# A two-layer hybrid diffusion block on one Trainium2 core: the prologue's loads, engine orders and first norm rearranged

## Chip, core and metric

One core of one Trainium2 chip runs the whole program in one launch. The metric is the device time of an execution in microseconds (us). TensorE multiplies (PE in the rows; PEld loads its weights), VectorE is DVE, ScalarE is ACT, GpSimd is POOL; SyncE (SP) only issues DMAs. A q behind an engine's name (SPq, ACTq) marks work of its sequencer.

## What is computed

Two layers over 256 context tokens and 256 latent tokens, D = 1024, all in float32. Cut to what the change touches:

```python
h = rmsnorm(x, norm_mix[i]) * (1 + sc1) + sh1        # sc1, sh1: silu(c) @ w_mod, per stream
... = split_in(h @ w_in[i])                          # three mixers and gates read h
# Hyena's filter, a function of the weights alone:
h = sin(fr * (emb @ w1 + b1)); h = sin(fr * (h @ w2 + b2))
h = (h @ w3) * exp(-t * decay)
k = concatenate([h[:, 0], 0, h[:0:-1, 1]])
k = k / sum(|k|);  k_f = rfft(k)
```

The rest (recurrent scan, Hyena convolutions, SSD, projections, SwiGLU, final norm) is the same in both kernels.

## The kernel before

Weights come as 128x1024 tiles (`wst`), are split into a high part `whi` (ScalarE) and a low part `wlo` (VectorE), and are multiplied with the split activations `hhi`, `hlo`; a planner (`Flow`) walks a list of weight tiles and steps the generators (`gens_step`) that do everything else between the products. A generator gives up the engine with `yield n`, so lags such as `FILT_LAG` set where its pieces stand. The order that results on each engine is a list in which every instruction waits for its operands; a scheduler may move instructions against the written order where nothing ties them.

Before the first weight tile of layer 0 stands a prologue (in `run`, under `if l == 0`):

- `silu_c`: silu of c, for both streams.
- `g_filters` and `filt`: two small sine layers (`sin_rr`, result `h2` in tile `nr`), then for each of four filter parts jp (tiles `w0` to `w3`, one PSUM pool each) four blocks `n`. A block is: ScalarE makes exp(decay), TensorE multiplies `h2` with `w3` of the part, VectorE multiplies the two, ScalarE takes the absolute value, VectorE adds it up. Then eight VectorE sums and differences, the sum over all taps (`ones` products, `kcol`), and five products with the cosine and sine basis `kbas`, copied by ScalarE and stored by a GpSimd DMA (`kd`).
- `mods0`: 16 tiles of `w_mod0` (`wm`) times silu(c), giving `modt` (shift and scale).
- `g_sumsq`: ScalarE squares x (`yc` context, `yl` latent) in 16 pieces, GpSimd adds them up in `nacc` (14 adds).
- `g_norm`: from `nacc` by TensorE, ScalarE (Sqrt) and VectorE (RECIPROCAL) the factor `rc`, spread over the partitions by TensorE; then per stream 8 pairs of VectorE operations with a ScalarE operation between them make `hhi` and `hlo`.

After that the first tiles, D and B0, are multiplied (`f.tile(2)`), and the filters' remains are drained. All loads of the prologue go through SyncE's queue, in this order: small constants, filter inputs, three tiles of `w_mod0`, x, the other 13 tiles (a ring of four).

An issue of a DMA on SyncE or ScalarE takes the next of eight completion counters (DMAHW0 to DMAHW7), whichever engine issues it, and waits until the DMA before it on the same counter has landed. GpSimd's have eight of their own (DMASW0 to 7).

Of the kernel before, what the change touches and what calls it, by code (L numbers as in the profile page):

```python
# [9 lines left out]
F32 = mybir.dt.float32  # L10
F32R = mybir.dt.float32r
AF = mybir.ActivationFunctionType
# [10 lines left out]
LATE = 2  # L23
FILT_LAG = ((2, 2, 0, 1, 1, 0, 2, 1), (8, 7, 1, 3, 2, 0, 4, 3))
MODSTEP = ((2, 2, 4, 3), (3, 2, 2, 2, 1, 1))
PREP_LAG = (17, 12)
MODLAGS = (3, 16, 6)
ORDER_A = ('D B0 C0 B1 C1 X0 X1 X2 X3 R0 R1 X4 X5 Z0 Z1 G0 G1 R2 R3 X6 X7 Z2 Z3 G2 G3 R4 R5 Z4 Z5 G4 G5 R6 R7 Z6 Z7 G6 G7 T20 T21', 'D B0 C0 B1 C1 X0 X1 X2 X3 R1 X4 R0 X5 Z0 G0 Z1 G1 R2 R3 X6 X7 Z2 Z3 H00 G2 G3 H01 R4 R5 Z4 Z5 G4 G5 H10 H11 R6 R7 Z6 Z7 G6 G7 H20 H21 T20 T21')
ORDER_B = ('H00 H20 H10 H01 H11 T22 H21 W20 H12 H02 W21 T23 H22 H03 H13 W22 T24 H04 H14 W23 H23 H24 H05 H15 T25 W24 T26 H25 H06 H16 W25 H17 T27 H26 H07 W26 H27 W27', 'H02 H03 H12 H13 H22 H23 W20 T22 W21 T23 W22 T24 W23 T25 W24 T26 H04 H05 W25 H15 T27 W26 W27 T00 H24 H14 H25 T01 W00 T02 W02 W01 H06 H07 T03 T04 W03 H16 H17 T05 T06 W05 H26 H27 W04 T07 W06 W07')
P = 128  # L30
# [177 lines left out]
class Block:  # L208
    def __init__(self, tc, a, out, es):
        self.tc = tc  # L210
        self.nc = tc.nc
        self.a = a
        self.out = out
        self.es = es
        self.f = Flow(self)
        self.ring = (3, 2)
        self.l = 0
        self.table, self.before, self.group = None, [], []

    def pool(self, name, bufs=1, space=None, es=None):  # L220
# [9 lines left out]
    def mm(self, out, lhsT, rhs, start=True, stop=True):  # L230
        self.nc.tensor.matmul(out=out, lhsT=lhsT, rhs=rhs, start=start, stop=stop)  # L231

# [36 lines left out]
    def tt(self, out, in0, in1, op, eng=None):  # L269
        (eng or self.nc.vector).tensor_tensor(out=out, in0=in0, in1=in1, op=op)  # L270

    def stt(self, out, in0, scalar, in1, op0, op1):
        self.lastop = self.nc.vector.scalar_tensor_tensor(out=out, in0=in0, scalar=scalar, in1=in1, op0=op0, op1=op1).ins.name  # L273

    def ts(self, out, in0, s1, op0, s2=None, op1=None):
        if op1 is None:
            self.nc.vector.tensor_scalar(out=out, in0=in0, scalar1=s1, scalar2=None, op0=op0)
        else:
            self.nc.vector.tensor_scalar(out=out, in0=in0, scalar1=s1, scalar2=s2, op0=op0, op1=op1)

# [73 lines left out]
    def silu_c(self):  # L354

        t = self.t
        self.sil = t(self.cp, [P, KT, 2], "sil")
        self.act(self.sil.rearrange("p k s -> p s k"), self.cs.rearrange("p (s k) -> p s k", s=2), AF.Silu)
        silc = self.t(self.wm, [P, KT, 32], "silc")
        self.nc.vector.memset(silc, 0.0)  # L360
        self.act(silc[:, :, 0:2], self.sil)
        self.silc = silc

        row = t(self.base, [P, T], "btmp", bufs=3)[0:4]
        self.nc.sync.dma_start(out=row, in_=self.a["crow"])
        self.act(row, row, AF.Silu)
        self.sild = t(self.dram, [4, T], "sild")
        self.nc.sync.dma_start(out=self.sild, in_=row)

# [5 lines left out]
    def mods0(self, qs):  # L375

        todo = [(q, k) for q in qs for k in range(KT)]
        sts = []

        def load(i):  # L380
            if i < len(todo):
                st = self.t(self.wm, [P, KT * P], "wm", bufs=4)
                self.nc.sync.dma_start(out=st, in_=self.a["w_mod0"][todo[i][0], todo[i][1]])
                sts.append(st)

        ahead = 3
        for i in range(ahead):
# [59 lines left out]

    def rms_r(self, sq_sum, n, f=1.0, keep=True):

        nb = n // P  # L450
        ps = self.pc()
        for b in range(nb):
            self.mm(ps[:, b:b + 1], sq_sum[:, b * P:b * P + P], self.ones[:, 0:1])
        rc = self.t(self.base, [P, 4], "rc")
        self.act(rc[:, 0:nb], ps[:, 0:nb], AF.Sqrt, bias=self.epsc, scale=f / D)
        self.nc.vector.reciprocal(out=rc[:, 0:nb], in_=rc[:, 0:nb])
        ps = self.pc()
        for b in range(nb):
            self.mm(ps[:, b * P:b * P + P], rc[:, b:b + 1].to_broadcast([P, P]), self.ident)
        if not keep:  # L460
            return ps
        r = self.t(self.base, [P, T], "nr")
        self.act(r[:, 0:n], ps[:, 0:n])
        return r
# [16 lines left out]
    def g_sumsq(self, x, acc):  # L481
        yield 6
        for k in range(KT):
            self.sq_acc(acc, k, [x[0][:, k], x[1][:, k]], eng=self.nc.gpsimd)
            yield 1

    def g_norm(self, l, xs, mi, acc, qsh, wname, out, wait=None):
# [11 lines left out]
        if not wait:  # L499
            r = self.rms_r(acc, NTOK * len(xs), keep=False)  # L500
        for s, x in enumerate(xs):
            sl = slice(s * NTOK, s * NTOK + NTOK)
            if wait:
                if s:
                    yield wait, s
                ra = self.rms_r(acc[:, sl], NTOK, keep=False)[:, 0:NTOK]
            else:
                ra = r[:, sl]
            for k in range(KT):
                tmp = self.t(self.base, [P, T], "btmp", bufs=3)[:, 0:NTOK]  # L510
                sh = mod[:, qsh, k, mi[s]:mi[s] + 1]
                self.stt(tmp, x[:, k], am[:, k, mi[s]:mi[s] + 1], ra, ALU.mult, ALU.mult)
                self.act(hi[:, k, sl], tmp, AF.Identity, bias=sh)
                self.stt(lo[:, k, sl], tmp, sh, hi[:, k, sl].bitcast(F32), ALU.add, ALU.subtract)
                if k % 2:
                    yield 1
        if qsh:
            self.after = self.lastop
            self.f.mark(("normed", l))
# [447 lines left out]
    def sin_rr(self, x, q, outs):  # L967

        big = 12582912.0
        self.ts(q, x, 1.0 / (2.0 * math.pi), ALU.mult)  # L970
        self.ts(q, q, big, ALU.add)
        self.ts(q, q, big, ALU.subtract)
# [7 lines left out]
    def g_filters(self, l, fp, sets=None):  # L980
# [4 lines left out]
        emb = t(fp, [P, T], "emb")[0:33, 0:NTOK] if one else t(fp, [33, NTOK], "emb")  # L985
        self.wmq.dma_start(out=emb, in_=a["emb"])
        w1 = t(fp, [33, 64], "fw1")
        self.wmq.dma_start(out=w1, in_=a["hy_w1"][l])
        w2 = t(fp, [64, 64], "fw2")
        self.wmq.dma_start(out=w2, in_=a["hy_w2"][l])  # L990
        kbas = t(fp, [P, 5, P], "kbas")
# [48 lines left out]
    def filt(self, l, jp, fp, kbas, h2, sl, ks, pool, ptag):  # L1040
# [17 lines left out]
        for n, (d, ti) in enumerate(((0, 0), (0, 1), (1, 0), (1, 1))):  # L1058
# [7 lines left out]
            h = hv[ti, d]  # L1066
            if n == 0 and self.fspl:
                self.act(s0[0:1], ps[0:1])
                for b in range(4):
                    nc.sync.dma_start(out=kc[:, 8 + b:9 + b], in_=s0[0:1, b * P:b * P + P])  # L1070
            if ti == 0:
# [24 lines left out]
        for b in range(4):  # L1096
            self.mm(pt[:, b:b + 1], acc[:, b * P:b * P + P], self.ones[:, 0:1])
            if not self.fspl:
                self.mm(pt[:, 4 + b:5 + b], w3[:, b * P:b * P + P], h2[:, 0, 0:1])
        inv, cb, k0 = kc[:, 0:4], kc[:, 4:8], kc[:, 8:12]  # L1100
        if not self.fspl:
            self.act(k0, pt[:, 4:8])
        self.act(inv, k0, AF.Abs)
# [335 lines left out]
    def run(self):  # L1439
# [9 lines left out]
        for l in range(DEPTH):  # L1449
# [8 lines left out]
            with ExitStack() as ls:  # L1458
# [6 lines left out]
                if l == 0:  # L1465
                    self.wm = self.pool("wm0", es=st)
                    self.wmq = nc.sync
                    self.silu_c()
                    fp = self.pool("fl0", es=st)
                    sets = []  # L1470
                    for i in range(4):
                        w = t(fp, [P, 11, T], f"w{i}")
                        sets.append(([w[:, k] for k in range(6)], w[:, 6:11]) +
                                    ((self.ps_a, "a"), (self.ps_c, "c"), (self.ps_mm, "mm"), (self.ps_mm, "mm"))[i])
                    f.spawn(self.g_filters(0, fp, sets))
                    f.gens_step()
                    g = f.spawn(self.mods0((1, 0)))
                    f.gens_step()
                    for s in range(2):
                        nc.sync.dma_start(out=x[s], in_=self.a["x"][s])  # L1480
                    sq = f.spawn(self.g_sumsq(x, acc))
# [3 lines left out]
                if l == 0:  # L1485
                    f.spawn(self.g_norm(0, x, (0, 1), acc, 0, "norm_mix", self.h_tiles))
                f.drain([g[0] for g in f.gens])
                f.drain(self.fgens)
                st.close()
                self.sb, self.mh, self.ml, self.vh, self.vl = {}, [], [], {}, {}  # L1490
                if last:
                    self.hp_pool = self.pool("hp", es=ls)
                with self.tc.tile_pool(name=f"ssd{l}", bufs=1) as self.ssd_pool, \
# [15 lines left out]
                    if last:  # L1509
                        self.spawn_parts(0, (0, 1), n)  # L1510
                    f.tile(2)
                    f.run(("gt", 2, 1))
# [221 lines left out]
```

## Time and profile before

| | us |
|---|---|
| median of three runs (2065.45 to 2067.81) | 2066.91 |
| the profiled execution's own time | 2069.64 |
| its span, first to last instruction | 2067.9 |
| TensorE busy | 1989.1 (96%) |
| VectorE busy | 1497.8 (72%) |
| ScalarE busy | 1021.3 (49%) |
| GpSimd busy | 275.1 (13%) |

Busy times are unions of the instructions of an engine over the span; matmuls are pipelined and their ends are modelled, so 96% does not say that TensorE runs at its peak. "Idle before" names what ended a wait. Times in the rows count from the first instruction.

### The profile page before, as it was taken

Reading aid. Unit: us, or ns where it says so; the run is one execution under the profiler, and the core shown is the slowest. Engines: PE = TensorE matmul, PEld = TensorE weight load, DVE = VectorE, ACT = ScalarE, POOL = GpSimd, SP = SyncE. Lnnn points to the kernel's source line nnn. Section 1 sums busy time; section 2 is a strip of 40 time slices with the busy share of each in tenths; the row PEclk is TensorE's granted clock in tenths of the full one; section 3 lists DMA queues with packets and bytes.
Section 4 is the critical chain, followed back from the end, with each engine's and each line's share of the span. In section 5 each row is a group of like instructions: output and inputs, shape, how many; then the busy total and the mean of one; then the engine's idle time right before and its main releaser. Section 6 shows DMA issues by size and latency. Waiting matters only on the chain.

```text
span 2067.9 us, 30071 instructions
## 1 busy us (share of the span) xinstructions
PE 1989.1 (96%) x11564; PEld 1693.7 (82%) x11564; DVE 1497.8 (72%) x2422; ACT 1021.3 (49%) x1602; POOL 275.1 (13%) x330
## 2 busy tenths in 40 slices
PE   7999899899999999999999999999999899999998
PEld 3797767678888887888877888897767899999998
DVE  7786765697777789469988455787676898765555
ACT  6556658752222323344424435556768644455444
POOL 3103232220000112011121000003242110000000
PEclk9999999999999999999999999999999999999999
DMA  7621122243232377345686423532233565455563
GB/s 270 221 82 60 60 71 67 87 153 115 89 100 82 123 264 258 109 133 193 204 289 236 133 88 108 152 93 92 79 96 108 186 208 167 154 188 155 184 184 112
DMA packets 84743, 297.15 MB, mean 144 GB/s; under 512 B 12650, under 2 KB 13894, under 8 KB 83193
## 3 DMA queue, kind: packets, MB, share of 16 engines
q1 hardware_dynamic: 61208, 208.40, 31.6%
q0 software_dynamic: 22848, 86.32, 12.6%
q8 instruction: 91, 1.49, 0.3%
q10 hardware_dynamic: 544, 0.52, 0.1%
q14 instruction: 52, 0.42, 0.1%
HBM read 278.41 MB, written 16.79 MB: 143 GB/s over the span
## 4 chain that ended last, share of the span: by engine, by line
PE 72%; issue 9%; DVE 7%; ACT 4%; DMA 4%; POOL 2%; SPq 0%; POOLq 0%; DVEq 0%; ACTq 0%
PE mm L231 61%; PE c L231 6%; PE b L231 3%; PE a L231 2%; DMA wm<-in_w_modt 2%; DVE wlo L270 1%; PE c L246 1%; ACT L259 1%; ACT r L259 1%; POOL r L270 1%; POOL wm L422 1%; DVE r L942 1%; DVE w L270 1%; ACT whi L259 1%; DVE r L937 1%
## 5 line engine op out<-in xcount | busy, mean ns | idle before, releaser
L259 ACT ACTIVATE whi<-wst 128x1024 fp32r<-128x1024 f32 (+1 forms) x374 | 392.5, 1050 | 524.9 <-PE mm L231 423.0
L270 DVE TENSOR_TENSOR wlo<-wst,whi 128x1024 fp32r<-128x1024 f32 (+1 forms) x374 | 456.6, 1221 | 250.2 <-PE mm L231 121.0
L231 PE MATMUL mm<-hhi,whi 128*128 128x256 f32 (+1 forms) x1552 | 504.9, 345 | 14.8 <-DVE u L273 6.8
L231 PE MATMUL mm<-hlo,whi 128*128 128x256 f32 (+1 forms) x1552 | 490.8, 336 | 0.2
L231 PE MATMUL mm<-shi,whi 128*128 128x256 f32 (+1 forms) x1104 | 351.1, 338 | 3.2 <-ACT shi L259 3.2
L231 PE MATMUL mm<-slo,whi 128*128 128x256 f32 (+1 forms) x1104 | 350.9, 338 | 1.7 <-DVE slo L270 0.7
L231 PEld LDWEIGHTS mm<-hhi,whi 128*128 128x128 f32 x1552 | 294.8, 190 | 53.1 <-issue 17.1
L231 PEld LDWEIGHTS mm<-hlo,whi 128*128 128x128 f32 x1552 | 295.4, 191 | 34.8 <-issue 7.9
L231 PE MATMUL mm<-hhi,wlo 128*128 128x256 f32 (+1 forms) x1552 | 304.0, 336 | 0.1
L231 PEld LDWEIGHTS mm<-hhi,wlo 128*128 128x128 f32 x1552 | 241.0, 189 | 32.5 <-issue 5.2
L231 PEld LDWEIGHTS mm<-shi,whi 128*128 128x128 f32 x1104 | 210.4, 192 | 26.6 <-ACT shi L259 5.2
L231 PEld LDWEIGHTS mm<-slo,whi 128*128 128x128 f32 x1104 | 210.7, 192 | 24.3 <-DVE slo L273 1.7
L231 PE MATMUL mm<-shi,wlo 128*128 128x256 f32 (+1 forms) x1104 | 213.7, 336 | 0.9 <-DVE wlo L270 0.9
L231 PEld LDWEIGHTS mm<-shi,wlo 128*128 128x128 f32 x1104 | 174.4, 192 | 22.2 <-DVE wlo L270 1.4
L437 DVE SCALAR_TENSOR_TENSOR wmp<-wm,silr 128x1024 f32<-128x1024 f32 x128 | 156.0, 1219 | 20.8 <-DMA wm<-in_w_modt 19.9
L231 PE MATMUL mm<-vl,whi 128*128 128x256 f32 (+1 forms) x508 | 156.7, 330 | 0.0
L231 PE MATMUL mm<-vh,whi 128*128 128x256 f32 (+1 forms) x508 | 156.2, 330 | 0.0
L231 PEld LDWEIGHTS mm<-vl,whi 128*128 128x128 f32 x508 | 96.4, 190 | 9.9 <-DVE vl L270 0.2
L259 ACT ACT_TABLE_LOAD x78 | 100.1, 1283 | 8.9 <-PE c L231 5.3
L231 PEld LDWEIGHTS mm<-vh,whi 128*128 128x128 f32 x508 | 96.2, 190 | 9.8 <-ACT vh L259 0.6
L231 PE MATMUL mm<-vh,wlo 128*128 128x256 f32 (+1 forms) x508 | 97.5, 332 | 0.0
L231 PEld LDWEIGHTS mm<-vh,wlo 128*128 128x128 f32 x508 | 79.3, 192 | 9.6
(322 smaller groups left out, 2670.8 us busy)
## 6 DMA issues: line engine op xcount, KB each, us to landing
wst<-in_w_in SPq DMA_DIRECT2D x170, 512.0 KB, 3.6
wst<-in_w_up SPq DMA_DIRECT2D x88, 512.0 KB, 3.6
wm<-in_w_modt POOLq DMA_DIRECT2D x80, 512.0 KB, 4.8
wst<-in_w_branch SPq DMA_DIRECT2D x48, 512.0 KB, 3.6
wst<-in_w_down SPq DMA_DIRECT2D x32, 512.0 KB, 3.6
ks<-kd POOLq DMA_DIRECT2D x16, 640.0 KB, 7.1
wst<-in_w_out SPq DMA_DIRECT2D x18, 512.0 KB, 3.6
wm<-in_w_mod SPq DMA_DIRECT2D x16, 512.0 KB, 4.7
```

The lines of the kernel that those rows point to most:

```text
L231: self.nc.tensor.matmul(out=out, lhsT=lhsT, rhs=rhs, start=start, stop=stop)
L246: self.nc.tensor.transpose(out, in_, self.ident[0:n, 0:n])
L259: ins = self.nc.scalar.activation(out=out, in_=in_, func=func, **kw).ins
L270: (eng or self.nc.vector).tensor_tensor(out=out, in0=in0, in1=in1, op=op)
L422: self.nc.gpsimd.dma_start(out=st, in_=self.a["w_modt"][l, todo[i][0], todo[i][1]])
L437: ins = self.nc.vector.scalar_tensor_tensor(out=out, in0=sts[i], scalar=1.0, in1=self.silr[:, s], op0=ALU.mult, op1=ALU.mult, accum_out=do ...
L937: nc.vector.tensor_tensor_scan(out=h, data0=av, data1=i[:, 0], initial=0.0, op0=ALU.mult, op1=ALU.add)
L942: nc.vector.tensor_tensor_scan(out=h[:, sl][:, ::-1], data0=av[:, sl][:, ::-1], data1=i[:, 1, sl][:, ::-1], initial=ini, op0=ALU.mult, op1 ...
```

## The change

Parts, in the order of the program:

1. x is loaded first, by ScalarE's queue; `kbas`, the filter's `w3` and decays too (`wmq = nc.scalar`). SyncE's queue keeps the small constants and `w_mod0`; 12 tiles of it are issued ahead of use instead of 3, eight of them into the space of `hlo` and `hhi`, which nothing uses yet. The store of `sild` goes to GpSimd's queue.
2. In the prologue every matmul is tied behind the one written before it, and every VectorE operation made by `tt`, `stt`, `ts` too (`told`, `chain`): these two engines follow the written order. Lags change.
3. `rms_r` of layer 0 moves to the end of `g_sumsq`, its result is copied to a tile `r0`.
4. `g_norm` writes its second VectorE operation one step later; it is run after three steps and drained, and the filter parts 2 and 3 wait for the norm of stream 0 and 1 before their sums. D and B0 are multiplied inside the prologue, before the filters are drained.
5. `sin_rr` does its multiply and add in one operation (two instead of three).
6. The filter's tap 0 (`k0`) is copied from the first block's product by ScalarE and spread over partitions by four GpSimd DMAs per part, instead of four `nr` x `w3` products per part.

The diff, cut to its core:

```diff
+NORM_LAG = 3
-FILT_LAG = ((2, 2, 0, 1, 1, 0, 2, 1), (8, 7, 1, 3, 2, 0, 4, 3))
+FILT_LAG = ((1, 2, 0, 4, 1, 0, 1, 1), (8, 7, 1, 3, 2, 0, 4, 3))
-PREP_LAG = (17, 12)
-MODLAGS = (3, 16, 6)
+PREP_LAG = (14, 12)
+MODLAGS = (1, 16, 6)
...
+    def chain(self, engine, made):
+
+        if self.told is not None:
+            if engine in self.told:
+                self.order(made.ins, self.told[engine])
+            self.told[engine] = made.ins.name
+        return made
...
-        self.nc.sync.dma_start(out=self.sild, in_=row)
+        self.nc.gpsimd.dma_start(out=self.sild, in_=row)
...
+        big = [self.t(self.base, [P, KT, T], tag).rearrange("p (i k) n -> p i (k n)", i=4) for tag in ("hlo", "hhi")]
+        room = [b[:, i] for b in big for i in range(4)]
...
-                st = self.t(self.wm, [P, KT * P], "wm", bufs=4)
+                st = room[i - 4] if 4 <= i < 12 else self.t(self.wm, [P, KT * P], "wm", bufs=4)
...
-        ahead = 3
+        ahead = 12
...
+        self.r0 = self.rms_r(acc, T, out=self.t(self.wm, [P, T], "r0"))
...
-            r = self.rms_r(acc, NTOK * len(xs), keep=False)
+            r = self.r0
...
-        self.ts(q, x, 1.0 / (2.0 * math.pi), ALU.mult)
-        self.ts(q, q, big, ALU.add)
+        self.ts(q, x, 1.0 / (2.0 * math.pi), ALU.mult, big, ALU.add)
...
-            if n == 0 and self.fspl:
+            if n == 0:
                 self.act(s0[0:1], ps[0:1])
                 for b in range(4):
-                    nc.sync.dma_start(out=kc[:, 8 + b:9 + b], in_=s0[0:1, b * P:b * P + P])
+                    (nc.sync if self.fspl else gp).dma_start(out=kc[:, 8 + b:9 + b], in_=s0[0:1, b * P:b * P + P])
...
+        if not self.fspl and jp > 1:
+            yield ("normed0", jp - 2)
...
-            if not self.fspl:
-                self.mm(pt[:, 4 + b:5 + b], w3[:, b * P:b * P + P], h2[:, 0, 0:1])
...
-                    self.wmq = nc.sync
+                    self.wmq = nc.scalar
+                    for k in range(2):
+                        nc.scalar.dma_start(out=x[k], in_=self.a["x"][k])
...
-                    for s in range(2):
-                        nc.sync.dma_start(out=x[s], in_=self.a["x"][s])
...
-                    f.spawn(self.g_norm(0, x, (0, 1), acc, 0, "norm_mix", self.h_tiles))
+                    for i in range(NORM_LAG):
+                        f.gens_step()
+                    nm = f.spawn(self.g_norm(0, x, (0, 1), acc, 0, "norm_mix", self.h_tiles))
+                    f.drain([nm])
+                    f.tile(2)
```

What moves, at two places. First ScalarE at the start of the program. Before, it issues no DMA, and the first sine layer's Sin (`w_141<-w_141`) is its fifth ACTIVATE:

```order
L259 ACT_TABLE_LOAD
L259 ACTIVATE sil<-cs 128x2x8
L259 ACTIVATE btmp<-btmp 4x512
L259 ACTIVATE silc<-sil 128x8x2
L259 ACTIVATE sp_sc<-sp_nl 128x16
L259 ACTIVATE w_141<-w_141 64x256
L259 ACTIVATE nr<-w_141 64x256 x2
L259 ACT_TABLE_LOAD
```

With the change (the Sin is now `w_146<-w_146`; w_146, w_143, w_145, w_144 are the four filter parts; the counter that each waits for in brackets):

```order
L1014 DMA kbas<-in_kbas 128x640 [waits DMAHW4_49]
L1059 DMA w_146<-in_hy_w 128x512 [waits DMAHW5_49]
L1060 DMA w_146<-in_hy_decay 128x1024 [waits DMAHW7_49]
L1059 DMA w_143<-in_hy_w 128x512 [waits DMAHW1_49]
L1060 DMA w_143<-in_hy_decay 128x1024 [waits DMAHW2_49]
L1059 DMA w_145<-in_hy_w 128x512 [waits DMAHW4_49]
L1060 DMA w_145<-in_hy_decay 128x1024 [waits DMAHW6_49]
L1059 DMA w_144<-in_hy_w 128x512 [waits DMAHW0_49]
L1060 DMA w_144<-in_hy_decay 128x1024 [waits DMAHW1_49]
L269 ACTIVATE w_146<-w_146 64x256 [waits DVE_49]
```

Nine DMA issues now stand in ScalarE's list ahead of that Sin (two for x ahead of these, as the very first). The counters behind the brackets: DMAHW7 is held by the latent half of x, DMAHW1 and DMAHW2 by the second and third tile of `w_mod0`, DMAHW6 by the fifth, DMAHW0 by the context half of x, then the first tile and then the sixth.

Second GpSimd, between the loads and the store of the first filter part. Before:

```order
L321 DMA pp_87<-in_cols 128x336
L321 DMA pp_90<-in_cols 128x336
L270 ISA
L270 TENSOR_TENSOR nacc<-nacc,btmp 128x256 x14
L1125 DMA kd_111<-w_141 128x2560
```

With the change:

```order
L381 DMA sild<-btmp 4x512
L280 ISA
L280 TENSOR_TENSOR nacc<-nacc,btmp 128x256 x2
L1092 DMA kcol_119<-w_146 128x1x1 x4
L1092 DMA kcol_119<-w_143 128x1x1 x4
L1092 DMA kcol_119<-w_145 128x1x1 x4
L1092 DMA kcol_119<-w_144 128x1x1 x4
L280 TENSOR_TENSOR nacc<-nacc,btmp 128x256 x12
L1145 DMA kd_111<-w_146 128x2560
```

The sixteen issues for `k0`, which need the first block of every filter part, stand between the second and the third add of `nacc`.

## Rows read from the trace of the kernel before

**Rows 1.** Stretches: busy time (instructions) of each engine, PEclk granted clock.

```profile
core 0: us, PE busy (x) PEld busy (x) DVE busy (x) ACT busy (x) POOL busy (x), PEclk, DMA share, GB/s
0.00:10.00 10.00, 1.44 (x3) 0.57 (x4) 4.50 (x16) 2.87 (x6) 1.98 (x7) 1.00 0.63 176
10.00:20.00 10.00, 5.70 (x15) 1.68 (x14) 4.37 (x10) 5.95 (x10) 0.00 (x0) 1.00 1.03 415
...
60.00:70.00 10.00, 8.97 (x14) 3.39 (x14) 6.10 (x15) 4.56 (x9) 0.00 (x0) 0.66 0.64 223
...
80.00:90.00 10.00, 10.00 (x76) 9.76 (x75) 5.96 (x13) 4.44 (x9) 1.37 (x3) 1.00 0.64 252
...
160.00:170.00 10.00, 10.00 (x60) 8.21 (x59) 6.43 (x7) 7.59 (x12) 4.59 (x4) 1.00 0.17 52
...
14.85:85.07 70.22, 66.07 (x345) 34.20 (x345) 58.90 (x116) 48.87 (x100) 16.71 (x18) 0.93 0.71 268
```

**Rows 2.** Timeline, 2 to 17 us: start, length, engine, operation [idle before].

```profile
2.39 0.22 ACT L259 ACTIVATE sil<-cs 128x16 f32<-128x16 f32 x1 [0.37 <-DMA cs<-in_cc]
...
9.17 0.42 ACT L259 ACTIVATE w<-w 64x256 f32<-64x256 f32 x1 [4.06 <-DVE w L279]
...
13.99 0.86 ACT L259 ACTIVATE nr<-w 64x256 f32<-64x256 f32 x2 [4.41 <-DVE w L279]
...
14.87 1.28 ACT L259 ACT_TABLE_LOAD   x1
...
16.16 1.95 ACT L259 ACTIVATE w<-w,misc 128x512 f32<-128x512 f32 x3
```

**Rows 3.** SyncE's queue, 0 to 90 us: what its issues waited for, us, times, longest.

```profile
SPq L383 <- DMA w<-in_hy_decay: 2.3, 2, 1.4
```

**Rows 4.** DMA queues in the last 14 us, where SyncE and ScalarE both issue.

```profile
q1 hardware_dynamic: 544, 0.52, 11.3%
q10 hardware_dynamic: 544, 0.52, 11.0%
```

**Rows 5.** Tile nacc, 0 to 95 us: ns min/median/max of one, first and last start.

```profile
L270 POOL TENSOR_TENSOR nacc<-nacc,btmp x14: 722/1174/1245, 26.7 to 47.5; 128x256 f32<-128x256 f32 x14
```

**Rows 6.** GpSimd's groups, 0 to 95 us: busy, mean ns of one, idle before.

```profile
L1125 POOL DMA_DIRECT2D kd<-w x4 | 2.2, 545 | 31.1 <-ACT w L259 31.1
```

**Rows 7.** Timeline, 48 to 77 us: the norm's factor, and the first tile's first product.

```profile
48.13 1.16 PE L231 MATMUL c<-ones,nacc 128*128 128x1 f32 x8
...
49.42 1.28 ACT L259 ACT_TABLE_LOAD   x1
...
50.71 0.26 ACT L259 ACTIVATE rc<-c,epsc 128x4 f32<-128x4 f32 x1
...
66.96 0.17 DVE L456 RECIPROCAL rc<-rc 128x4 f32<-128x4 f32 x1
...
75.85 0.68 PE L231 MATMUL mm<-hhi,whi 128*128 128x256 f32 x1
```

**Rows 8.** Timeline of VectorE, 36 to 85 us: sums, low parts, first and last norm step.

```profile
36.13 2.48 DVE L270 TENSOR_TENSOR w<-w 128x512 f32<-128x512 f32 x4
...
64.61 2.36 DVE L270 TENSOR_TENSOR wlo<-wst,whi 128x1024 fp32r<-128x1024 f32 x2
...
71.15 1.26 DVE L273 SCALAR_TENSOR_TENSOR btmp<-yc,am,c 128x256 f32<-128x256 f32 x3 [4.02 <-PE c L231]
...
84.59 0.48 DVE L273 SCALAR_TENSOR_TENSOR hlo<-btmp,modt,hhi 128x256 fp32r<-128x256 f32 x1 [0.18 <-ACT hhi L259]
```

**Rows 9.** Tile w, 0 to 92 us: ScalarE's operations and the basis products.

```profile
L259 ACT ACTIVATE w<-w x17: 416/614/631, 9.2 to 55.7; 128x512 f32<-128x512 f32 x16, 64x256 f32<-64x256 f32 x1
L259 ACT ACTIVATE w<-w,misc x16: 705/707/722, 16.2 to 48.7; 128x512 f32<-128x512 f32 x16
L259 ACT ACTIVATE w<-mm x10: 582/597/598, 61.5 to 75.6; 128x512 f32<-128x512 f32 x10
```

**Rows 10.** Chain that ended last, 0 to 160 us: start, length, what.

```profile
77.73 0.94 PE c L231 x2
...
79.51 0.98 PE c L231 x2
80.49 12.19 PE mm L231 x94
92.67 0.39 PE c L246 x4
```

More of the change, by code (lines that the diff above doesn't have):

```diff
@@ L218, in __init__ @@
         self.table, self.before, self.group = None, [], []
+        self.told = None
     def pool(self, name, bufs=1, space=None, es=None):
@@ L230, in mm @@
     def mm(self, out, lhsT, rhs, start=True, stop=True):
-        self.nc.tensor.matmul(out=out, lhsT=lhsT, rhs=rhs, start=start, stop=stop)
+        self.chain("PE", self.nc.tensor.matmul(out=out, lhsT=lhsT, rhs=rhs, start=start, stop=stop))
     def mm3(self, out, lhsT, rhs):
@@ L269, in tt @@
     def tt(self, out, in0, in1, op, eng=None):
-        (eng or self.nc.vector).tensor_tensor(out=out, in0=in0, in1=in1, op=op)
+        made = (eng or self.nc.vector).tensor_tensor(out=out, in0=in0, in1=in1, op=op)
+        if eng is None:
+            self.chain("DVE", made)
     def stt(self, out, in0, scalar, in1, op0, op1):
-        self.lastop = self.nc.vector.scalar_tensor_tensor(out=out, in0=in0, scalar=scalar, in1=in1, op0=op0, op1=op1).ins.name
+        made = self.nc.vector.scalar_tensor_tensor(out=out, in0=in0, scalar=scalar, in1=in1, op0=op0, op1=op1)
+        self.lastop = self.chain("DVE", made).ins.name
     def ts(self, out, in0, s1, op0, s2=None, op1=None):
         if op1 is None:
-            self.nc.vector.tensor_scalar(out=out, in0=in0, scalar1=s1, scalar2=None, op0=op0)
+            self.chain("DVE", self.nc.vector.tensor_scalar(out=out, in0=in0, scalar1=s1, scalar2=None, op0=op0))
         else:
-            self.nc.vector.tensor_scalar(out=out, in0=in0, scalar1=s1, scalar2=s2, op0=op0, op1=op1)
+            self.chain("DVE", self.nc.vector.tensor_scalar(out=out, in0=in0, scalar1=s1, scalar2=s2, op0=op0, op1=op1))
     def col(self, name, i=0, n=1, rows=P):
@@ L445, in mods, with rms_r @@
                 self.tt(self.modts[l][:, q, :, s0:2], dot[:, :, s0:2], b, ALU.add)
-    def rms_r(self, sq_sum, n, f=1.0, keep=True):
+    def rms_r(self, sq_sum, n, f=1.0, keep=True, out=None):
         nb = n // P
@@ L461, in rms_r @@
             return ps
-        r = self.t(self.base, [P, T], "nr")
+        r = self.t(self.base, [P, T], "nr") if out is None else out
         self.act(r[:, 0:n], ps[:, 0:n])
@@ L508, in g_norm @@
                 ra = r[:, sl]
[L509 to L514, printed above, removed]
+            tmps = []
+            for k in range(KT + 1):
+                if k < KT:
+                    tmp = self.t(self.base, [P, T], "btmp", bufs=3)[:, 0:NTOK]
+                    tmps.append(tmp)
+                    sh = mod[:, qsh, k, mi[s]:mi[s] + 1]
+                    self.stt(tmp, x[:, k], am[:, k, mi[s]:mi[s] + 1], ra, ALU.mult, ALU.mult)
+                    self.act(hi[:, k, sl], tmp, AF.Identity, bias=sh)
+                if k:
+                    sh = mod[:, qsh, k - 1, mi[s]:mi[s] + 1]
+                    self.stt(lo[:, k - 1, sl], tmps[k - 1], sh, hi[:, k - 1, sl].bitcast(F32), ALU.add, ALU.subtract)
                 if k % 2:
                     yield 1
+            if not wait:
+                self.f.mark(("normed0", s))
         if qsh:
@@ L985, in g_filters @@
         emb = t(fp, [P, T], "emb")[0:33, 0:NTOK] if one else t(fp, [33, NTOK], "emb")
-        self.wmq.dma_start(out=emb, in_=a["emb"])
+        (self.wmq if one else nc.sync).dma_start(out=emb, in_=a["emb"])
         w1 = t(fp, [33, 64], "fw1")
-        self.wmq.dma_start(out=w1, in_=a["hy_w1"][l])
+        (self.wmq if one else nc.sync).dma_start(out=w1, in_=a["hy_w1"][l])
         w2 = t(fp, [64, 64], "fw2")
-        self.wmq.dma_start(out=w2, in_=a["hy_w2"][l])
+        (self.wmq if one else nc.sync).dma_start(out=w2, in_=a["hy_w2"][l])
         kbas = t(fp, [P, 5, P], "kbas")
@@ L1097, in filt @@
             self.mm(pt[:, b:b + 1], acc[:, b * P:b * P + P], self.ones[:, 0:1])
-            if not self.fspl:
-                self.mm(pt[:, 4 + b:5 + b], w3[:, b * P:b * P + P], h2[:, 0, 0:1])
         inv, cb, k0 = kc[:, 0:4], kc[:, 4:8], kc[:, 8:12]
-        if not self.fspl:
-            self.act(k0, pt[:, 4:8])
         self.act(inv, k0, AF.Abs)
@@ L1473, in run @@
                         sets.append(([w[:, k] for k in range(6)], w[:, 6:11]) +
-                                    ((self.ps_a, "a"), (self.ps_c, "c"), (self.ps_mm, "mm"), (self.ps_mm, "mm"))[i])
+                                    ((self.ps_mm, "mm"), (self.ps_a, "a"), (self.ps_c, "c"), (self.ps_mm, "mm"))[i])
+                    sets = [sets[i] for i in (3, 0, 2, 1)]
+                    self.told = {}
                     f.spawn(self.g_filters(0, fp, sets))
@@ L1485, in run @@
                 if l == 0:
-                    f.spawn(self.g_norm(0, x, (0, 1), acc, 0, "norm_mix", self.h_tiles))
+                    for i in range(NORM_LAG):
[3 more added lines that the diff above has]
+                    f.tile(2)
                 f.drain([g[0] for g in f.gens])
                 f.drain(self.fgens)
+                self.told = None
                 st.close()
@@ L1510, in run @@
                         self.spawn_parts(0, (0, 1), n)
-                    f.tile(2)
+                    if last:
+                        f.tile(2)
                     f.run(("gt", 2, 1))
```

## The prediction

> **What bounds the kernel now.** I read the time by stretches first. From 80 us on TensorE is busy in the whole of every 10 us up to 170 us (the first and the last of these nine stretches stand in [rows 1]; the seven between read 10.00 too), so a prologue that ends later or sooner moves everything behind it by about as much. The prologue is another matter: VectorE has 4.50 and 4.37 us of work in the first two stretches of ten. So I followed its start in the timeline [rows 2]: the Sin of the first sine layer stands at 9.17, that of the second is through at 14.85, the table for Exp at 16.15, the first decay factor at 16.16. Then came the waits and the DMA queues [rows 3, 4], GpSimd's adds [rows 5], the factor of the norm [rows 7], VectorE's pace [rows 8], and last the chain [rows 10]: the first product of a weight tile starts at 75.85, and tiles D and B0 with all that remains of the filters end at 92.67. My question is when the changed kernel reaches these two points.
>
> **The change, step by step.**
>
> *1. ScalarE is held up by its own DMA issues.* The change puts nine of them ahead of the first Sin, and the last ones wait for counters held by weight tiles of SyncE's queue. That an issue stands still for a counter is seen on SyncE: twice, 2.3 us in all [rows 3]. The issue of the last part's w3 needs the sixth tile of w_mod0 to have landed. First the two halves of x pass, 2.10 MB: at the 415 GB/s of the stretch from 10 to 20 us, whose DMA share of 1.03 says that the engines are full [rows 1], 5.1 us, from a first issue at about 0.7 and 1.6 us to landing as for cs (0.74 to 2.39) [rows 2], some 7 us. Six tiles are 3.15 MB. Where SyncE's and ScalarE's queues ran side by side they had 11.3% and 11.0% [rows 4], an equal share; at half of 415 the tiles take 15.2 us and end at 22, at the full rate 7.6 us and end at 15. ScalarE's queue is empty for part of the time, since its own issues wait, but not for most: I take 21. The Sin goes from 9.17 to 21.3: 12 us late (bounds 6 and 13, and 0 if a waiting issue didn't hold the engine: a rival below).
>
> Beside this row stands the Trainium skill, "DMA: Bandwidth & Descriptors", section "Issuing engines are not separate DMA queues": transfers issued by different engines share the same 16 DMA engines and interleave, and a second issuer only saves issue time. By it, part 1 of the change gains no bandwidth, which the equal shares agree with; if it gained some, the 21 would be nearer 15.
>
> *2. Up to the first decay factors.* From the first Sin to the end of the second took 5.7 us [rows 2]; one VectorE operation on 64x256 falls away in it, for which I take 0.3 (ScalarE's Sin on as many elements takes 0.42). So h2 is there at 26.7, and with 1.28 us for the table Exp begins at 28.0, 12 us late. All filter inputs have landed by then or soon after, the last being issued at 21.5.
>
> *3. First blocks.* ScalarE now does an Exp (0.71, 0.61 to the next) and a copy of tap 0 for each of four parts. The copy has no row: one partition of 512 elements lies between nothing and the 0.60 of a 128x512 copy [rows 9]; I take 0.5, nearest to the latter since the length is the same. Four pairs: 4.5 us, so the fourth copy is through at 32.8, the first at 29.2.
>
> *4. GpSimd.* Sixteen issues of about 0.54 us [rows 6] follow the first copy: 29.3 to 38. Behind them stand twelve adds of 0.72 to 1.25 us [rows 5]: through at 46.7 to 53. The longer ones belong to stretches in which VectorE was busy, and it now waits; I take 1.0 and 50. Before, the last add began at 47.5. ScalarE's squares share three buffers with these adds and stand in its list between the Exps, so the later blocks go at GpSimd's pace.
>
> *5. The norm's factor.* In the written order TensorE's product with nacc stands ahead of the fourth part's third block, and VectorE's RECIPROCAL ahead of its multiply. So VectorE stops there until nacc is complete: 1.16 for the products, 0.26 for the Sqrt, hand-overs of about 0.8 [rows 7], RECIPROCAL at 52.2 (before: 66.96, where nothing but the norm waited for it). The table goes back to Exp (1.28), an absolute value and an Exp follow, then VectorE's multiply: through at 56.
>
> *6. VectorE from there to the third part's last sum.* Counted in its list: 36 operations on 128x512 at 0.62 (four in 2.48), two low parts in 2.36, 23 of the norm's 32 steps at 0.435 (32 from 71.15 to 85.07), 13 small ones at 0.1 [rows 8]: 22.3 + 2.4 + 10.0 + 1.3 = 36 us, to 92.
>
> *7. TensorE from there.* Three basis products of 0.9 (two passes took 0.94 and 0.98 [rows 10]) with ScalarE's copies beside them stand ahead of tile D: first product at 94.5, against 75.85. That is **18.7 us late**.
>
> *8. Inside tiles D and B0* the changed kernel still has seven basis products and four with ones to do, the kernel before two: five times 0.9 and four of 0.22 make **5.2 us**. The sums of the fourth part, which they wait for, come within the time that the products take.
>
> *9. Behind them* ScalarE's list now has the split of a third weight tile ahead of the copy of tile D, which waits for another tile's products; 1.06 and 0.6 us and two hand-overs, **about 2 us** (0 to 2.5).
>
> *10. TensorE's clock.* In 60 to 70 us the granted clock was 0.66 of full, two thirds of that stretch at 1.2 GHz [rows 1], behind a stretch with waits. The changed kernel leaves TensorE without work for longer, some 8 us ahead of step 7: **1 us** (0 to 4).
>
> Gains, all hidden: 16 products of tap 0 fewer on TensorE (3.5 us), which waits anyway; x and w_mod0 there earlier, which nothing on the new path waits for except through step 1. The shift and scale leave the path.
>
> Sum: 18.7 + 5.2 + 2 + 1 = 27 us, nothing of it caught up later. Against the profiled execution's 2069.64, which is 2.7 above the median, that is 2096.6; against the median of 2066.91 it is **2094 us**. The bounds: adds at 0.72 and the sixth tile at 18 give 20 us, 2087; adds at 1.25, hand-overs in every dependent pair of sums (0.1 each, some 2 us) and 4 us of slow clock give 36 us, 2103.
>
> **Rivals.**
>
> *A. ScalarE isn't held up by waiting issues.* Then h2 is ready at 14.5, but the fourth part's decay still comes behind 5.6 MB of its own queue and as much of the other: about 27 us. The fourth copy ends near 29, its four issues near 31, the adds at 43, RECIPROCAL at 45: 7 us sooner than in the forecast, +20, 2087. For it: an issue is no work of the engine that the rows count as busy. Against it: rows 3 show SyncE's list in order behind a waiting issue. The Trainium skill, "Perfetto Trace Analysis", section "DMA Instruction — HWDGE (DVE, Sync)", has the semaphore wait in the sequencer, which is free for its next instruction only after the issue; by it this rival falls and the sum stands. Chance 0.12.
>
> *B. Faster: VectorE's gaps close.* From 14.85 to 85.07 VectorE was idle for 11.3 us (70.22 less 58.90 [rows 1]). If inputs come early enough, the written order fills half of that, and the fourth part's eight sums (5.0 us at 0.62) come behind the norm instead of ahead: tile D starts 10.6 us earlier, less 5.2 of step 8: 5 us gained, 2062. It decides at ScalarE's last issue: it would have to leave before about 9 us, with GpSimd's adds done by 44. Six tiles and x by then are 5.2 MB in 7 us, 750 GB/s, where rows 1 show 415. Chance 0.08.
>
> *C. The delay is made up* in the tile stage: 2067. Against it: TensorE has no gap there to give back [rows 1]. Chance 0.05.
>
> **How the numbers follow.** The forecast has 0.75. Rival A lies inside its range. 2079 to 2104 takes in its bounds, A, and a case between A and B in which both holds are shorter than priced. A measurement of this kernel tells about 0.2%, 4 us, from no change. Faster by more than that: B, 0.08. Within it: C, 0.05. Slower: 0.87.
>
> **What would show each step.** The first Sin near 21 us with DMA issues ahead of it on ScalarE; the first Exp near 28; sixteen issues on GpSimd and nacc's last add ending near 50; RECIPROCAL of rc near 52 with VectorE idle before it; the first tile product near 95 and the end of D and B0 near 117. A first Sin at 9 to 10 would leave A or B; nacc complete before 44 would take most of the rest away. A first tile product before 75 would make the forecast wrong as a whole.

## Result and profile after

The changed kernel takes 2091.36 us (median of four runs, 2089.10 to 2099.88) against 2067.36 (2065.45 to 2078.11): ratio 1.0124, 95% interval 1.0100 to 1.0148 (the two medians alone give 1.0116), slower by 24 us. The forecast was 2094 in a range of 2079 to 2104. The profiled execution took 2090.39 (span 2088.4).

ScalarE's timeline of the changed kernel, first and last of the nine issues and what follows them (start, length, engine, operation, idle before), answering to [rows 2]:

```profile
9.48 0.33 ACTq L1014 DMA_DIRECT2D kbas<-in_kbas  x1
...
20.51 0.34 ACTq L1059 DMA_DIRECT2D w<-in_hy_w  x1
21.78 0.33 ACTq L1060 DMA_DIRECT2D w<-in_hy_decay  x1
22.16 0.42 ACT L269 ACTIVATE w<-w 64x256 f32<-64x256 f32 x1 [14.30 <-DMA w<-in_hy_w]
...
27.16 0.85 ACT L269 ACTIVATE nr<-w 64x256 f32<-64x256 f32 x2 [3.25 <-DVE w L292]
28.03 1.28 ACT L269 ACT_TABLE_LOAD   x1
29.32 0.72 ACT L269 ACTIVATE w<-w,misc 128x512 f32<-128x512 f32 x1
```

The nine issues are 0.4 to 2.5 us apart. Of the last two, that at 20.51 follows the landing of the sixth tile of `w_mod0` at 20.49, and that at 21.78 the landing of ScalarE's own load of the second part's `w3` at 21.76 (issued at 12.63): in both cases the DMA before on the same counter. The Sin stands behind them with 14.30 us of idle time. GpSimd, VectorE and TensorE up to the first product of a weight tile, same view, answering to [rows 5 to 8]:

```profile
30.82 4.30 POOL L1092 DMA_DIRECT2D kcol<-w  x8 [5.83 <-ACT w L269]
...
41.00 9.16 POOL L280 TENSOR_TENSOR nacc<-nacc,btmp 128x256 f32<-128x256 f32 x12
...
45.46 1.60 DVE L280 TENSOR_TENSOR w<-w 128x512 f32<-128x512 f32 x1 [1.54 <-ACT w L269]
...
47.65 1.25 DVE L280 TENSOR_TENSOR w<-w 128x512 f32<-128x512 f32 x1
...
51.30 0.16 DVE L471 RECIPROCAL rc<-rc 128x4 f32<-128x4 f32 x1
...
53.71 0.75 DVE L285 SCALAR_TENSOR_TENSOR w<-a,misc,w 128x512 f32<-128x512 f32 x1 [1.34 <-ACT w L269]
...
85.77 0.48 DVE L285 SCALAR_TENSOR_TENSOR hlo<-btmp,modt,hhi 128x256 fp32r<-128x256 f32 x1 [0.18 <-ACT hhi L269]
...
91.75 2.74 DVE L280 TENSOR_TENSOR w<-w 128x512 f32<-128x512 f32 x4
92.49 0.50 PEld L233 LDWEIGHTS c<-w,kbas 128*128 128x128 f32 x2 [9.51 <-DVE w L280]
92.49 5.72 PE L233 MATMUL c<-w,kbas 128*128 128x512 f32 x6 [9.43 <-DVE w L280]
...
97.41 0.93 PE L233 MATMUL mm<-hhi,whi 128*128 128x256 f32 x1
```

The adds end at 50.16, the factor comes at 51.30. With the row at 85.77, through at 86.25, VectorE has the first stream's norm done, so the products of tile D with this stream could begin. TensorE stands 9.43 us at a basis product of the third filter part instead, whose last four sums VectorE writes from 91.75 on. The stretches show it, and the clock with it (columns as in [rows 1]):

```profile
60.00:70.00 10.00, 3.80 (x13) 2.14 (x13) 9.79 (x19) 3.90 (x10) 0.00 (x0) 0.69 0.32 105
70.00:80.00 10.00, 10.00 (x21) 4.81 (x22) 7.38 (x18) 3.50 (x7) 0.00 (x0) 0.63 0.01 2
80.00:90.00 10.00, 3.06 (x14) 1.78 (x12) 9.33 (x21) 5.81 (x13) 1.10 (x2) 0.88 0.62 262
90.00:100.00 10.00, 7.46 (x23) 3.95 (x24) 8.89 (x23) 4.50 (x9) 0.00 (x0) 0.61 0.00 0
...
160.00:170.00 10.00, 10.00 (x76) 9.73 (x75) 8.55 (x15) 5.89 (x9) 0.00 (x0) 1.00 0.18 55
```

Two low parts of weight tiles, of which the first starts behind D's last product and the second behind B0's; then ScalarE's copy of D and its transposes. VectorE, ScalarE and TensorE:

```profile
112.58 1.23 DVE L280 TENSOR_TENSOR wlo<-wst,whi 128x1024 fp32r<-128x1024 f32 x1 [6.95 <-PE mm L233]
116.81 1.23 DVE L280 TENSOR_TENSOR wlo<-wst,whi 128x1024 fp32r<-128x1024 f32 x1 [3.00 <-PE mm L233]
...
125.43 0.68 ACT L269 ACTIVATE w<-mm,pp 64x512 f32<-64x512 f32 x1 [1.66 <-DMA kd<-w]
...
126.16 0.46 PE L248 MATMUL c<-ident,w 64*128 64x64 f32 x4 [2.37 <-ACT w L269]
```

The same two, the third and the fourth, in the kernel before:

```profile
87.51 1.23 DVE L270 TENSOR_TENSOR wlo<-wst,whi 128x1024 fp32r<-128x1024 f32 x1 [2.44 <-PE mm L231]
90.87 1.22 DVE L270 TENSOR_TENSOR wlo<-wst,whi 128x1024 fp32r<-128x1024 f32 x1 [2.13 <-PE mm L231]
```

So the changed kernel is 25.1 us late behind D and 25.9 behind B0. The lateness doesn't stay there: the sixth low part is 30.4 late (134.8 against 104.3), the 49th 24.2 (500.9 against 476.7), which is what the medians differ by.

### The profile page after: what moved, and what is told of

Read it like the earlier page. It is cut to its first block, busy times and chain, and to the rows that moved or that the text cites. A ratio compares the mean times of both kernels' runs of the same rounds, so it can differ in the third digit from the quotient of the medians.

```text
span 2088.4 us, 30042 instructions
## 1 busy us (share of the span) xinstructions
PE 1987.9 (95%) x11532; PEld 1691.6 (81%) x11532; DVE 1499.5 (72%) x2418; ACT 1021.8 (49%) x1603; POOL 282.4 (14%) x347
## 3 DMA queue, kind: packets, MB, share of 16 engines
q0 software_dynamic: 23392, 86.34, 12.3%
```

## Experiments

Each is an edit of the changed kernel; times are medians, ratios stand against the kernel before, run beside it on the same chip. Differences between two edits are taken from the medians; where these come from two chips, the ratios can give a few us more or less.

**E1: filter inputs on SyncE's queue.**

```diff
-                    self.wmq = nc.scalar
+                    self.wmq = nc.sync
```

> The changed kernel with kbas and the filter's w3 and decays back on SyncE's queue (x stays on ScalarE's). Theory H (ScalarE's own issues hold up the prologue, as in step 1): the first Sin goes from 22.2 back to 9 to 10 us. All of its 12 us would show only if nothing else were late; TensorE's written order has products with w_mod0 ahead of the filter's first blocks, and these tiles now land behind 3.5 MB of filter inputs, so I expect about half: first product of a weight tile 97.4 - 6 = 91 us, time 2091 - 6 = 2085. Rival 1, the issues are the whole loss of the prologue: first product near 85, 2079. Rival 2, the hold-up is hidden behind GpSimd or VectorE: 2091, no change.

Measured: 2091.90, ratio 1.0114 (1.0098 to 1.0130): no change, so rival 2. The Sin went to 14.59 and `h2` to 19.27, 8 us sooner, and nothing came of it. Timelines of TensorE, GpSimd and VectorE in this kernel:

```profile
20.88 2.23 PE L233 MATMUL b<-wm,silc 128*32 128x256 f32 x16 [4.72 <-DMA wm<-in_w_mod]
...
38.39 8.24 POOL L280 TENSOR_TENSOR nacc<-nacc,btmp 128x256 f32<-128x256 f32 x12
```

```profile
39.82 7.37 DVE L280 TENSOR_TENSOR w<-w 128x512 f32<-128x512 f32 x1
...
47.77 0.68 DVE L280 TENSOR_TENSOR w<-w 128x512 f32<-128x512 f32 x1
...
51.38 0.18 DVE L471 RECIPROCAL rc<-rc 128x4 f32<-128x4 f32 x1 [0.41 <-ACT rc L269]
```

Two covers took the 8 us. TensorE waited for `w_mod0`, whose products the written order has ahead of the filter's blocks; and while GpSimd made its adds back to back (0.69 each), one sum of VectorE took 7.37 us in place of 0.68. The RECIPROCAL stands behind that sum: 51.38, as before the edit.

**E2: tap 0 by products again** (part 6 undone).

```diff
-            if n == 0:
+            if n == 0 and self.fspl:
...
+            if not self.fspl:
+                self.mm(pt[:, 4 + b:5 + b], w3[:, b * P:b * P + P], h2[:, 0, 0:1])
...
+        if not self.fspl:
+            self.act(k0, pt[:, 4:8])
```

> The changed kernel without its part 6: tap 0 again by four products of nr and w3 per part on TensorE, no k0 issues on GpSimd. Theory G (the sixteen issues hold up the adds of nacc, step 4): the adds run on from 23.6 at the pace of ScalarE's squares, the last ends near 45 to 47 in place of 50.2; the RECIPROCAL of rc, the first tile product and the time come 4 to 5 us earlier: 2086.5. Rival 1, all 10 us from 30.8 to 41 are lost to the issues: RECIPROCAL near 41, 2081. Rival 2, VectorE's work, not the factor, sets the first tile product: 2091, no change.

Measured: 2088.69, ratio 1.0101 (1.0086 to 1.0116). RECIPROCAL at 47.89, first tile product at 94.28: 3.4 and 3.1 us earlier. In the profile the direction is theory G's and the size two thirds of it; in the time 2.7 us, which the intervals don't separate from none.

**E3: both.**

> Both of the edits before, filter inputs on SyncE's queue and tap 0 by products. If the two hold-ups stand in series (step 1, then step 4) their gains add: 10 us, first tile product 87 to 88, 2081. If they are two covers of one delay, no more than the larger of the two: 2085. If they are all that the change cost, the time of the kernel before: 2067.

Measured: 2086.63, ratio 1.0086 (1.0070 to 1.0102); RECIPROCAL 45.16, first product 92.86. By the medians under 5 us of 24 come back, by the ratios 8. These two hold-ups aren't most of what the change cost.

**E4: no written order.**

```diff
-                    self.told = {}
```

> The changed kernel without its part 2 (the table told is not made, so neither TensorE nor VectorE is tied to the written order); ScalarE's issues and GpSimd's stay. My prediction's account, in which the order costs only VectorE's stop at the RECIPROCAL (52 to 56): 4 us back, 2087. Rival W, the written order is itself the larger part, because both engines stand behind waits that the scheduler would have stepped around (VectorE has 1.4, 2.8 and 3.1 us of work in the first three stretches of ten): first tile product near 80, 14 to 16 us back, 2076.

Measured: 2079.57, ratio 1.0053 (1.0036 to 1.0071): 11.8 us back by the medians, some 15 by the ratios, so nearest rival W. ScalarE's Sin is as late as in the changed kernel (22.60) and the RECIPROCAL even later (53.11), but TensorE goes to the weight tile before the third part's basis products (its timeline; compare 92.49 and 97.41 above):

```profile
70.51 10.46 PE L233 MATMUL mm<-w,kbas 128*128 128x512 f32 x18
80.81 0.95 PE L233 MATMUL c<-ones,w 128*128 128x1 f32 x8
81.61 0.36 PE L233 MATMUL mm<-hhi,whi 128*128 128x256 f32 x1
```

**E5 and E6: the order on TensorE alone, on VectorE alone.**

```diff
-        if self.told is not None:
+        if self.told is not None and engine == "PE":
```

(E6 with "DVE".)

> The changed kernel with TensorE alone tied to the written order; VectorE is free. Without any order the time was 2079.6, with both 2091.4, so 11.8 us are to be shared out. Theory T (TensorE's order carries them, because it puts the basis products of three filter parts, which wait for VectorE's sums, ahead of the first weight tile): no more than 3 us come back, 2089. Rival V (VectorE's order carries them, because it stands at the RECIPROCAL and behind the long sums): 9 us or more come back, 2081. If each holds the other up, both this and the next run give back less than half: 2087 here.

> The counterpart: VectorE alone tied to the written order, TensorE free. Theory T: first product of a weight tile near 83 and 8 us or more back, 2082. Rival V: no more than 3 us back, 2089. If each holds the other up: 2086.

Measured: TensorE tied 2089.71, ratio 1.0105 (1.0089 to 1.0122), first product 95.32; VectorE tied 2081.77, ratio 1.0066 (1.0049 to 1.0084), first product 83.90. Theory T on both counts: freeing TensorE gives 9.6 us of the 11.8, freeing VectorE 1.7. The size of TensorE's share is less sure than its lead: at the 49th low part of the profiled executions E4 has won 10.1 us, E6 5.4 and E5 1.0 against the changed kernel.

**E7 and E8: GpSimd's adds set aside, and left out** (both with E1's edit; both leave the sum of squares out of `nacc`). The edit of E7; E8 makes no add in its place:

```diff
+                to = acc if self.told is None else sq
-                self.tt(acc[:, sl], acc[:, sl], sq[:, sl], ALU.add, eng)
+                self.tt(to[:, sl], acc[:, sl], sq[:, sl], ALU.add, eng)
```

> Filter inputs on SyncE's queue (time 2091.9 with that alone), and GpSimd's 14 adds are still made, but write their own input tile, so that nothing is summed in nacc (the sum of squares is left out) and the factor of the norm waits for no add. In the kernel with that edit alone one of VectorE's sums on 128x512 took 7.37 us (0.68 elsewhere) just while GpSimd made its last adds. Theory P (GpSimd's adds keep VectorE's sums from running): the long sum stays, 5 us or more, everything behind it stays where it was, 2091. Rival F (the late factor is the loss, and the long sum is no loss of its own): RECIPROCAL near 45 and first tile product 6 us earlier, 2086.

> The same, but the 14 adds are left out altogether (the sum of squares holds only the first piece); the sixteen issues for k0 stay on GpSimd. Theory P: the sum takes 0.7, and what stands behind it comes 6.7 us earlier; first tile product 98.7 - 6.7 = 92, time 2085. Rival F: the same time as in the run with the adds set aside. Rival N (something later holds the prologue anyway, as TensorE's basis products): 2091.

Measured: E7 2088.97, ratio 1.0104 (1.0088 to 1.0120); E8 2086.60, ratio 1.0086 (1.0065 to 1.0107). E7, GpSimd, VectorE and ScalarE:

```profile
38.19 9.70 POOL L280 TENSOR_TENSOR btmp<-nacc,btmp 128x256 f32<-128x256 f32 x12
```

```profile
40.01 0.91 DVE L280 TENSOR_TENSOR w<-w 128x512 f32<-128x512 f32 x1
...
46.37 0.93 DVE L280 TENSOR_TENSOR w<-w 128x512 f32<-128x512 f32 x1 [2.97 <-ACT w L269]
...
49.89 0.18 DVE L471 RECIPROCAL rc<-rc 128x4 f32<-128x4 f32 x1 [1.33 <-ACT rc L269]
```

```profile
45.41 0.42 ACT L269 ACTIVATE btmp<-yl 128x256 f32<-128x256 f32 x1 [0.27 <-POOL btmp L280]
45.73 1.13 ACT L269 ACTIVATE w<-w 128x512 f32<-128x512 f32 x2
```

And E8, VectorE:

```profile
40.71 0.68 DVE L280 TENSOR_TENSOR w<-w 128x512 f32<-128x512 f32 x1
...
46.83 0.18 DVE L471 RECIPROCAL rc<-rc 128x4 f32<-128x4 f32 x1 [0.43 <-ACT rc L269]
```

In E7 the long sum is gone although as many adds run: against theory P as I wrote it. Rival F had the RECIPROCAL near 45 and 6 us back; it came at 49.89, and 2.9 came back. What remains is another path: ScalarE's squares wait for buffers that the adds free, and the absolute values behind them in its list come late (2.97 us of VectorE's idle time). Without any adds (E8) the RECIPROCAL is at 46.83, the first product at 91.41, and 5.3 us come back against E1, near P's 6.7. So the adds cost some 5 us here on one path or the other; which of the two engines gives way differs between E1 and E7, and why is open.

**E9: the place of part 4 undone** (holds taken away, norm spawned as before, D and B0 behind the filters' remains; all of it still under the written order).

```diff
-            yield ("normed0", jp - 2)
...
-                    nm = f.spawn(self.g_norm(0, x, (0, 1), acc, 0, "norm_mix", self.h_tiles))
-                    f.drain([nm])
-                    f.tile(2)
+                    f.spawn(self.g_norm(0, x, (0, 1), acc, 0, "norm_mix", self.h_tiles))
...
+                if l == 0:
+                    f.tile(2)
```

> The changed kernel with part 4 undone as far as the place of D and B0 goes: the norm is spawned as before, the filter parts 2 and 3 don't wait for it, D and B0 are multiplied once the filters are drained. My step 8 has the products that stand inside D and B0 cost 5.2 us, and the trace shows 2.4 us more in which ScalarE's copy of D waits for the store of the last filter part. If these were losses of their own, 6 to 7 us come back: 2085. If they only stand where they would have stood ahead of D anyway (the fourth part's sums, 5.3 us on VectorE, then come ahead of D): no change, 2090 to 2091. Slower by those sums: 2096.

Measured: 2093.73, ratio 1.0139 (1.0116 to 1.0162), first product at 113.02. Nothing comes back, so what stands inside D and B0 is no loss of its own. Between no change and slower the time leaves it open. In the profiled execution the 49th low part comes 6.7 us behind the changed kernel's (507.6 against 500.9), near the third case, and the 373rd 0.7 behind.

**E10: no written order, filter inputs on SyncE's queue** (E4 and E1).

> No written order (2079.6 with that alone) and the filter inputs on SyncE's queue. With the order, the inputs' queue made no difference, since TensorE stood at the products with w_mod0 and VectorE at a long sum. If the order was the cover, the 18 us by which h2 comes sooner (32.2 to about 14) now show in part: k0's issues near 16 to 26, first tile product near 76, 4 to 5 us back, 2075. If GpSimd's adds and VectorE's amount of work set the end anyway: 2079 to 2080. If ScalarE's queue was the rest of the loss: 2067.

Measured: 2077.17, ratio 1.0057 (1.0037 to 1.0076), first product 82.09; `h2` at 19.07. 2.4 us against E4, which the intervals don't separate from none, between the first two cases. ScalarE's decays didn't move: the last starts at 59.0, in E4 at 59.2 (below).

**E11: E10 with lags near those of the kernel before.**

```diff
-FILT_LAG = ((1, 2, 0, 4, 1, 0, 1, 1), ...
+FILT_LAG = ((2, 2, 0, 1, 2, 0, 2, 1), ...
-MODLAGS = (1, 16, 6)
+MODLAGS = (4, 16, 6)
```

> The run before, with FILT_LAG = (2, 2, 0, 1, 2, 0, 2, 1) and MODLAGS = (4, 16, 6), nearly those of the kernel before; parts 3 to 6 of the change stay. What is left against the kernel before is then only what the change meant to do: norm ahead of the last filter parts, tap 0 by copy, one operation less per sine. If the lags carry the rest of the loss: the factor of the norm near 50, first tile product near 60 to 65 and D and B0 done a few us sooner than before, 2062 (bounds 2058 and 2067). If the order of work between the tiles is VectorE's total anyway: 2067. If GpSimd's issues and adds still hold VectorE up as in the runs with the order: 2072.

Measured: 2062.02 (2058.34 to 2065.61, eleven runs), ratio 0.9981 (0.9969 to 0.9993): 29 us faster than the changed kernel and 3 faster than the kernel before, the latter by an interval that ends just under 1. ScalarE's decays in E10, then in E11 (ns min/median/max, first and last start), and E11's first product:

```profile
L269 ACT ACTIVATE w<-w,misc x16: 704/706/721, 21.2 to 59.0; 128x512 f32<-128x512 f32 x16
```

```profile
L269 ACT ACTIVATE w<-w,misc x16: 704/707/721, 21.4 to 49.8; 128x512 f32<-128x512 f32 x16
```

```profile
64.65 0.37 PE L233 MATMUL mm<-hhi,whi 128*128 128x256 f32 x1
```

The filter's sixteen blocks take 9.2 us less. That fits the fourth entry of FILT_LAG, the steps between the two halves of a block, which is 1 again in place of 4; the four entries that differ and MODLAGS were not tried apart, nor the lags with the written order left in place. The norm's factor doesn't explain it: the RECIPROCAL comes at 54.80, later than in the changed kernel (51.30) and than expected (near 50). The first product comes 11 us before that of the kernel before (75.85), and much of that lead goes again inside D and B0, where filter work still stands: the third low part starts at 83.57, 3.9 us earlier.

**E12: E11 with the inputs on ScalarE's queue again.**

> The kernel of the run before (no written order, older lags, 2062), with one thing put back as in the change: kbas and the filter's w3 and decays go through ScalarE's queue. Under the written order this made no difference (2091.9 against 2091.4). Theory C (ScalarE's waiting issues do hold the prologue up by the 12 us of my step 1, and the written order and GpSimd's adds only covered it): h2 near 32 in place of 19.2, first tile product 10 to 12 us later than 64.7, time 2073 to 2076. Rival U (a waiting issue on ScalarE never cost anything, VectorE's total sets the end): 2062 to 2064.

Measured: 2071.23, ratio 1.0032 (1.0022 to 1.0043): 9.2 us slower than E11 by the medians, 10.5 by the ratios, nearest theory C. ScalarE and TensorE:

```profile
22.31 0.42 ACT L269 ACTIVATE w<-w 64x256 f32<-64x256 f32 x1 [14.38 <-DMA w<-in_hy_w]
...
31.54 0.85 ACT L269 ACTIVATE nr<-w 64x256 f32<-64x256 f32 x2 [2.54 <-DVE w L292]
```

```profile
78.04 0.36 PE L233 MATMUL mm<-hhi,whi 128*128 128x256 f32 x1
```

`h2` comes 12.3 us later than in E11 (19.24), the first product 13.4. Of the 12.3, the Sin has 7.8 (22.31 against 14.55); the rest comes behind it, where TensorE makes products with `w_mod0` up to 26.1 ahead of the second sine layer's. The hold-up that cost nothing in E1 costs 9 us once nothing covers it.

## Why the prediction was right, and where it was not

The total and most places came near the forecast; the cause was in part another, and some terms were right by luck:

| | forecast | measured |
|---|---|---|
| first Sin (step 1) | 21.3 | 22.16 |
| first decay factor (2) | 28.0 | 29.32 |
| issues for `k0` (4) | 29.3 to 38 | 30.82 to 41.0 |
| last add ends (4) | 50 | 50.16 |
| RECIPROCAL (5) | 52.2 | 51.30 |
| third part's last sum ends (6) | 92 | 94.49 |
| first tile product (7) | 94.5 | 97.41 |
| lateness behind B0's products (7, 8) | 23.9 | 25.9 |
| lateness at the sixth low part (7 to 10) | 26.9 | 30.4 |
| lateness at the 49th low part | 26.9 | 24.2 |

**Steps 1 and 2** held as a mechanism: a ScalarE issue that waits for a counter holds what stands behind it, and rival A fell with the Sin at 22.16. With two queues loading, the rate was 409, 418 and 404 GB/s in the stretches from 10 to 40 us, where [rows 1] has 415 with SyncE's loads alone. This agrees with what the Trainium skill says of shared engines in "DMA: Bandwidth & Descriptors", section "Issuing engines are not separate DMA queues". But my chain reads as if these 12 us were the first 12 of the loss. E1 and E12 show them worth nothing under the written order and 9.2 us without it: I followed one chain and didn't ask what would end last if its first link were gone.

**Steps 3 and 4** were right in place, and the 50.16 of the last add was right by luck: the issues ended 3 us later than forecast, at 41.0, and the twelve adds took 9.16 us in place of 12. Undone (E2), the adds end 4 us sooner (46.01), the RECIPROCAL comes 3.4 sooner, and some 3 us come back. Nor did the factor set tile D by itself: in E11 it comes later and D 33 us sooner. (The fourth copy's 32.8 is 0.3 more than step 3's own terms give; nothing hangs on it.)

**Step 5** had VectorE idle ahead of the RECIPROCAL; it wasn't. Its sums were stretched by the adds (1.60 and 1.25 in place of 0.68) and filled that time.

**Step 6** was short by 4 us: from the multiply behind the factor (through at 54.46) to the third part's last sum took 40, not 36; 2.32 of it is one wait for ScalarE's first `hhi` behind the copies of the basis products, which ran at a granted clock of 0.50 up to 77.4. The multiply had come 1.5 sooner than step 5 put it, so that only 2.5 show in the table.

**Step 7 is where the cause was put wrong.** It has three basis products "ahead of tile D" and prices them as 2.7 us of work, as though everything before were lateness of VectorE. E4 to E6 show that the tie itself is worth 11.8 us of 24, most of it TensorE's: VectorE had the first stream ready at 86.25, and in E6, with VectorE alone tied, TensorE starts D at 83.90. The lags, to which no step gives a price, are worth still more where they could be seen, 15 us between E10 and E11. Undone one after the other, order, queue and lags give 11.8, 2.4 and 15.2 us, more than the 24: E11, which keeps the rest of the change, is faster than the kernel before. The change also gives the filter parts other PSUM pools (`sets`), which no run undid.

**Step 8** has the right work inside, seven basis products and four with ones; from the first product to the end of B0 the lateness grew by 4.4 us, where it had 5.2 (its own terms, five of 0.9 and four of 0.22, make 5.4). Its mark was misread: 92.67 before is not the end of D and B0, whose last products end at 90.8, but the transposes of D's copy behind them. **Step 9** had a wrong reason: the copy of D waits for the store of the last filter part, whose space it takes (1.66 us on ScalarE, 2.37 on TensorE), not for the split of a weight tile. It had 2 us; between the fourth and the sixth low part the lateness grew by 4.5.

**Step 10** had 1 us for the clock, which was too little. From 92.49 to 97.90, behind the wait of 9.43 us, the granted clock was 0.50 (1.2 GHz), and the six basis matmuls took 5.72 us; six in the kernel before, at 1.00, took 2.74 (from 73.67). The eighteen from 71.24, at 0.72, took 11.04, where E11 at 1.00 took 7.99.

The sum of 27 us had "nothing of it caught up later". In the traces 30.4 were lost up to the sixth low part, and 6.2 were caught up by the 49th; so the total came near 24 with more lost and some given back. Rivals B and C fell: the first product came after 75, and 24.2 us were left at the 49th low part.

## What to carry to other kernels

A written order on an engine turns each wait for an operand into a wait of everything behind it: write it from the times at which operands come, and put work that is ready (here tile D) ahead of work that waits for a busy engine; such an order was not tried here. A DMA issue in ScalarE's list stood still for its completion counter, and the Sin behind it with it; here the loads did better in SyncE's list, which has no other work. Give lags a price like any other part of a change: here, between E10 and E11, they were the largest. Several late things on one path hide each other, so undoing one tells its worth only for that surrounding: E1 and E12 turn on the same line and find 0 and 9 us.

## What was not expected of the hardware

One VectorE sum of two 128x512 operands in SBUF, 0.68 us alone, took 7.37 us in E1 while GpSimd made twelve adds in 8.24 us, and 1.23 to 1.60 in the changed kernel, where VectorE's operations with one operand in PSUM, between these sums, kept their 0.74. With no adds (E8) it took 0.68 at the same place. The Trainium skill, "SBUF — State Buffer", section "Who interferes with whom", has a VectorE operation with two inputs in SBUF contend with a GpSimd operation that reads SBUF, over the read interface that they share, under an exclusive lock. The 7.37 us are longer than one such operation: some ten adds of 0.69 passed before the sum ended, 0.6 us behind the last of them.

Spans of single executions are a coarse ruler here: from the 97th low part to the 373rd, where all fourteen profiled kernels of this document run the same work, they took 1244.6 to 1254.0 us. A few us in the prologue are better read at a mark soon behind it, such as the 49th low part above.
